# GLA's decay differences as TensorE products with 0/1 masks, instead of scans and subtractions

## The chip, the cores and the metric

The kernel runs on one core of a Trainium2 chip. The metric is the device time of one execution in microseconds (us). Five engines work side by side: PE (TensorE, matmuls), DVE (VectorE), ACT (ScalarE), POOL (GpSimd) and SP, which only issues DMAs. Each takes its instructions in the order in which they stand in its own queue and waits at the head of that queue until its operands are there. TensorE's clock has two levels, 1.2 and 2.4 GHz; the profile gives the share of full speed that was granted.

## The reference, cut to what matters

Two layers of a hybrid backbone run over 384 tokens (128 context tokens, 256 latent ones). Each layer is a feed-forward part, a token mixer with three branches (Mamba-2 SSD, GLA, RWKV-7), and a second feed-forward part. The change is in the GLA branch. It has 4 heads with 64 key and 128 value channels, runs forward and backward, and works in chunks of 64 tokens:

```
lg = log_sigmoid(lr @ gla_gk_w[d] + gla_gk_b[d]) / 16        # a log decay per token and key channel
bc = cumsum(lg, within the chunk)
A[t, s] = sum_k q[t, k] * k[s, k] * exp(bc[t, k] - bc[s, k])  for s <= t
q_dec = q * exp(bc);  k_dec = k * exp(bc[last] - bc)
S_next = exp(bc[last]) * S + k_dec^T v                        # state from chunk to chunk
o = A v + q_dec S
```

The backward scan does the same on reversed tokens, and the two outputs are added.

## The kernel before, in words

Activations are feature-major: a tile holds 128 features by 384 tokens, so two GLA heads lie in one tile and the four heads make two head pairs (`hp`). The weights of the large products are split into a high and a low part (`wh`, `wl`: ACT casts, DVE subtracts) and every product of a 128x128 block is three matmuls of 128x384. In the mixer these read `psd<-mhh,wh` while the input is projected, and `psd<-ob,wh` while a branch's output goes through its output weights; each of the three branches (`w_rw_o`, `w_gla_o`, `w_ssd_o`) has 96 of them, and what PSUM then holds is gated into `merged` by DVE.

`mixer_` (L754) first projects and runs RWKV-7. Then `gla_decays` (L1733) makes the log decays, between the last projections. `scans` (L811) then runs GLA and SSD side by side in lanes that `pace` (L897) interleaves: `states(0)`, `states(1)` and `levels` of `gla` (L1701), and the lanes of SSD. The 96 products of `w_rw_o` are put between their steps; a further lane adds those of `w_gla_o` once GLA is done, and those of `w_ssd_o` come after all of it. `pace` orders the steps by a running model of each engine's time, and a scheduler then sets the final order, so that any new cost moves many instructions.

In GLA, `gla_decays` makes for each head pair and direction a product with the gate weights (`gk`, into PSUM), Abs, Exp and Ln on ACT, two steps on DVE (`gdm`), and a scan on DVE (`b`, one of four tiles) that sums the log decays within each chunk. `gla_states` (L1777) takes two exponentials of it (`qe`, `ke`), multiplies them by q and k (`glqk`), and carries the states `gS` from chunk to chunk.

`gla_levels` (L1832) makes the matrix A without large exponents. It halves the chunk six times. A level takes, for each block of 2H tokens, the pairs (t, s) on different sides of the block's middle, and measures both decays from that middle. Per head pair and level that is four differences into `gD` (two of 128x192 on DVE, two on POOL), one exponential of 128x768 on ACT, one product with q on DVE, one with k on POOL, twelve 64x64 matmuls, and a masked copy of 128x384 on DVE (`gA<-kt,psm`) which writes this level's pairs into A. The diagonal needs no decay.

`gla_output` (L1880) adds A times v and the state terms, and normalises. The matmuls of all these take PSUM from one pool of five banks (`psm`), the large products from another of two (`psd`). All mixer instructions bear line L275, that of the recorder through which they are issued, so they are told apart by their tiles. The lines that build a level's operands are these:

```
nc.vector.tensor_tensor(out=DQ[:, :, 1], in0=f4[:, :, 1], in1=mf, op=ALU.subtract)
nc.gpsimd.tensor_tensor(out=DK[:, :, 0], in0=mf, in1=f4[:, :, 0], op=ALU.subtract)
nc.scalar.activation(out=DD, in_=DD, func=AF.Exp, scale=1.0 / 16)
nc.vector.tensor_mul(out=DD[:, 0], in0=DD[:, 0], in1=q)
nc.gpsimd.tensor_mul(out=DD[:, 1], in0=DD[:, 1], in1=k)
```

## Time and profile before

| what | value |
|---|---|
| median of three runs | 2456.63 us (2456.47 to 2457.42) |
| the profiled execution, device time | 2458.13 us |
| its span in the trace | 2456.4 us, so 1.73 us lie outside it |
| mean granted TensorE clock | 0.97 of full speed |
| PE busy | 2311.0 us of the span (94%) |
| DVE busy | 1760.4 us (72%) |
| ACT busy | 1107.7 us (45%) |
| POOL busy | 509.6 us (21%) |

The profiled execution is 1.50 us above the median. "Busy" counts instructions alone, not DMA issues or semaphores; matmul ends are modelled, and a record can last longer than the distance to the next. The stretch in which GLA and SSD run side by side, from the first SSD and GLA products after the projections to the first products of `w_ssd_o` that run without a break, is 761.8 to 909.6 us in the first layer and 1956.5 to 2109 us in the second. For the first layer it is cut into four parts here: part 1, with the `w_rw_o` products (761.8 to 812.5), part 2, the rest of the second head pair's levels (812.5 to 836.8), part 3, the second head pair's states and outputs (836.8 to 857), and part 4, the rest of SSD, with the `w_gla_o` products (857 to 909.6).

### The profile page before, as it was taken

The page shows a single profiled execution, that of the slowest core. Times are in us where ns is not written, and L with a number is a line of the kernel's source. Part 1 is how long each engine was busy: PE and PEld are TensorE (multiplying, and loading weights), DVE is VectorE, ACT ScalarE, POOL GpSimd, SP SyncE. Part 2 cuts the span into 40 slices and gives each one's busy share as a digit, 9 for nine tenths or more (in the row PEclk, how much of TensorE's full clock was granted, in tenths as well). Part 3 has the DMA queues.
Part 4 walks back from the last instruction along what each step waited for, and adds up shares of the span by engine and source line. Part 5 has one row for each costly group of instructions (what it writes and reads, how often), then busy time and mean ns, then how long its engine had stood idle before and what let it go on. Part 6 is the DMA issues. An engine that isn't in the chain of part 4 may idle for free. (4 is left out here: it accounts for less than half of the span.)

```text
span 2456.4 us, 48779 instructions
## 1 busy us (share of the span) xinstructions
PE 2311.0 (94%) x19825; PEld 2132.9 (87%) x19825; DVE 1760.4 (72%) x3152; ACT 1107.7 (45%) x2015; POOL 509.6 (21%) x582
## 2 busy tenths in 40 slices
PE   6999899899998879999999999989999988999998
PEld 4999897888887669999999999978888766899998
DVE  3967769786658787868486877896767597885433
ACT  3533346354436445543345334744544544463322
POOL 3100024112215541100120001441212265220000
PEclk8999999999999989999999999989999988999999
DMA  9767554334425226667455766433433430554432
GB/s 304 239 201 210 171 156 111 95 96 124 115 83 143 62 73 202 179 189 219 130 183 165 229 211 163 137 83 104 115 106 107 121 113 16 175 180 131 129 117 80
DMA packets 501663, 354.14 MB, mean 144 GB/s; under 512 B 40035, under 2 KB 479985, under 8 KB 500927
## 3 DMA queue, kind: packets, MB, share of 16 engines
q1 hardware_dynamic: 496288, 337.44, 46.8%
q0 software_dynamic: 3680, 6.18, 1.2%
q10 hardware_dynamic: 1471, 7.41, 0.8%
q8 instruction: 155, 2.54, 0.4%
q14 instruction: 69, 0.57, 0.1%
HBM read 326.59 MB, written 24.38 MB: 143 GB/s over the span
## 5 line engine op out<-in xcount | busy, mean ns | idle before, releaser
L649 ACT CAST wh<-wraw 128x1024 fp32r<-128x1024 f32 (+2 forms) x296 | 280.1, 956 | 587.5 <-issue 332.4
L650 DVE TENSOR_TENSOR wl<-wraw,wh 128x1024 fp32r<-128x1024 f32 (+2 forms) x296 | 330.4, 1124 | 220.5 <-ACT wh L649 220.2
L662 PE MATMUL psm<-xh,wl 128*128 128x384 f32 (+1 forms) x896 | 305.2, 341 | 6.0 <-DVE wl L650 6.0
L660 PE MATMUL psm<-xh,wh 128*128 128x384 f32 (+1 forms) x896 | 306.4, 342 | 0.7 <-DVE xh L608 0.7
L661 PE MATMUL psm<-xl,wh 128*128 128x384 f32 (+1 forms) x896 | 304.2, 339 | 0.0
L275 DVE TENSOR_TENSOR wl<-wraw,wh 128x512 fp32r<-128x512 f32 x324 | 241.7, 758 | 84.2 <-ACT wh L275 77.4
L275 PE MATMUL psd<-mhh,wh 128*128 128x384 f32 x848 | 293.3, 347 | 6.1 <-DVE sb L275 3.4
L275 PE MATMUL psd<-mhl,wh 128*128 128x384 f32 x848 | 296.5, 350 | 2.6 <-DVE mhl L275 2.6
L275 PE MATMUL psd<-mhh,wl 128*128 128x384 f32 x848 | 295.3, 348 | 1.3 <-issue 1.3
L275 ACT CAST wh<-wraw 128x512 fp32r<-128x512 f32 x324 | 190.2, 614 | 166.9 <-PE psd L275 112.5
L536 DVE SCALAR_TENSOR_TENSOR aacc<-wada,cs,aacc 128x1024 f32<-128x1024 f32 x210 | 260.7, 1277 | 6.1 <-DMA wada<-in_w_ada_dram 5.7
L662 PE MATMUL psd<-gh,wl 128*128 128x384 f32 x704 | 237.0, 337 | 7.8 <-DVE wl L650 7.8
L660 PE MATMUL psd<-gh,wh 128*128 128x384 f32 x704 | 236.9, 336 | 0.0
L661 PE MATMUL psd<-gl,wh 128*128 128x384 f32 x704 | 236.5, 336 | 0.0
L621 POOL TENSOR_TENSOR acc<-acc,sq 128x384 f32<-128x384 f32 x24 | 28.9, 1205 | 719.6 <-ACT sq L619 710.3
L662 PEld LDWEIGHTS psm<-xh,wl 128*128 128x128 f32 x896 | 169.5, 189 | 8.4 <-DVE wl L650 8.4
L660 PEld LDWEIGHTS psm<-xh,wh 128*128 128x128 f32 x896 | 169.7, 189 | 6.2 <-issue 4.8
L275 PEld LDWEIGHTS psd<-mhl,wh 128*128 128x128 f32 x848 | 161.1, 190 | 15.3 <-issue 6.8
L275 PEld LDWEIGHTS psd<-mhh,wh 128*128 128x128 f32 x848 | 161.2, 190 | 15.0 <-issue 7.2
L660 PE MATMUL psm<-gh,wh 128*128 128x384 f32 x512 | 171.8, 336 | 0.0
L662 PE MATMUL psm<-gh,wl 128*128 128x384 f32 x512 | 171.1, 334 | 0.0
L661 PE MATMUL psm<-gl,wh 128*128 128x384 f32 x512 | 171.0, 334 | 0.0
(454 smaller groups left out, 4902.8 us busy)
## 6 DMA issues: line engine op xcount, KB each, us to landing
wada<-in_w_ada_dram SPq DMA_DIRECT2D x144, 512.0 KB, 4.6
wraw<-in_w_in_dram SPq DMA_DIRECT2D x112, 512.0 KB, 3.8
wraw<-in_ffn_gate_dram SPq DMA_DIRECT2D x88, 512.0 KB, 4.4
wraw<-in_ffn_up_dram SPq DMA_DIRECT2D x88, 512.0 KB, 4.5
wraw<-in_ffn_down_dram SPq DMA_DIRECT2D x64, 512.0 KB, 3.7
wraw<-in_ffn_down_dram SPq DMA_DIRECT2D x32, 384.0 KB, 4.8
gate<-sa SPq DMA_DIRECT2D x48, 192.0 KB, 2.3
gate<-gate SPq DMA_DIRECT2D x48, 192.0 KB, 2.5
```

The lines of the kernel that those rows point to most:

```text
L275: r = f(*a, **k)
L536: nc.vector.scalar_tensor_tensor(out=acc[:, c], in0=w, scalar=x, in1=acc[:, c], op0=ALU.mult, op1=ALU.add)
L621: (nc.vector if k == KD - 1 else nc.gpsimd).tensor_tensor(out=self.acc, in0=self.acc, in1=sq, op=ALU.add)
L649: nc.scalar.copy(out=h[:, x], in_=r[:, x])
L650: nc.vector.tensor_sub(out=lo[:, x], in0=r[:, x], in1=h[:, x])
L660: nc.tensor.matmul(ps, wh, xh, start=first, stop=False)
L661: nc.tensor.matmul(ps, wh, xl, start=False, stop=False)
L662: nc.tensor.matmul(ps, wl, xh, start=False, stop=last)
```

## The change

Log decays are now token-major: a tile holds 128 rows, 64 tokens of a chunk in both directions, by six chunks and 256 channels, split into a high and a low part (`lgh`, `lgl`). Every sum of log decays that GLA needs, from a block's middle to a token or from a token to the chunk's end, is a product of them with a matrix of zeros and ones (`gsum`, 128x1024, a new input that is built beside the constants). `gla_sum` makes one PSUM bank of such sums with four matmuls of 128x256: two chunks, the high and the low part each, and per chunk four groups of 64 columns. ACT takes the exponential out of PSUM.

- `gla_decays` makes twelve products of 64 tokens by 256 channels, four to a bank, instead of four of 128 channels by 384 tokens, adds the bias by DVE from a tile broadcast by DMA (`gkb`), and splits the result. The scans go. POOL issues three DMAs more: `gsum` (512 KB), ahead of the gate weights, and two for `gkb`.
- `gla_inter`, new, makes the decays to the chunk's ends for a head pair: three `gla_sum`, the totals `gtot` by two small copies, and the products with k on DVE and q on POOL, all in one tile `gE`. `gla_states` and `gla_output` read that tile.
- `gla_levels` goes in nine stages per head pair: three pairs of levels, three pairs of chunks. A stage has one `gla_sum`, one exponential of 128x512, a product with q on DVE and one with k on POOL (128x256 each), eight 64x64 matmuls, and two masked copies of 128x128. Three stages are prepared ahead (four buffers of `gD`). The subtractions on DVE and POOL go.

On DVE, while the `w_rw_o` products run, before: `b` are the summed decays, `gA` the matrix A, `merged` the gated output.

```order
L275 COPY_PREDICATED gA<-kt,psm 128x384
L275 TENSOR_TENSOR ke<-ke,glqk 128x384
L275 TENSOR_TENSOR gD<-b_8324 128x24x8
L275 TENSOR_TENSOR gD<-b_8328 128x24x8
L275 COPY_PREDICATED gA<-kt,psm 128x384
L275 TENSOR_TENSOR gD<-b_8324 128x48x4
L275 TENSOR_TENSOR gD<-b_8328 128x48x4
L275 TENSOR_TENSOR gD<-gD,glqk 128x384
L275 SCALAR_TENSOR_TENSOR merged<-gate,psd 128x384
```

On DVE at the same place after: `gE` is the tile of `gla_inter`, `sR` and `sD` belong to SSD.

```order
L294 TENSOR_TENSOR gE<-gE,glqk 128x6x64 x2
L294 COPY_PREDICATED gA<-kt,psm 128x128
L294 TENSOR_TENSOR gD<-gD,glqk 128x4x64
L294 COPY_PREDICATED gA<-kt,psm 128x128
L294 SCALAR_TENSOR_TENSOR merged<-gate,psd 128x384
L294 TENSOR_TENSOR sR<-adh,kt 128x512 x2
L294 COPY_PREDICATED gA<-kt,psm 128x128
L294 SCALAR_TENSOR_TENSOR sD<-kt,dt,sD 128x128
```

The subtractions `gD<-b` are gone, each 128x384 masked copy has become pieces of 128x128, and the multiply is 128x4x64.

On PE, where SSD's first products `ssi` and `ad` stand, before: `gD` are a level's 64x64 matmuls, `psd<-ob` the `w_rw_o` products.

```order
L275 MATMUL psm<-gD 64x64 x12
L275 MATMUL psm<-kt,ke 64x64 x12
L275 MATMUL psd<-ob,wh 128x384
L275 MATMUL psm<-kt,ke 64x64 x12
L275 MATMUL psm<-kt,ssi 64x128 x8
L275 MATMUL psm<-ad,kt 128x8 x8
L275 MATMUL psm<-gD 64x64 x12
L275 MATMUL psd<-ob,wl 128x384
```

On PE around the same two products after; all 96 `w_rw_o` products now stand ahead of this place.

```order
L294 MATMUL psm<-gD 64x64 x8
L294 MATMUL psm<-gsum,lgh 128x256
L294 MATMUL psm<-gsum,lgl 128x256
L294 MATMUL psm<-kt,ssi 64x128 x8
L294 MATMUL psm<-ad,kt 128x8 x8
L294 MATMUL psm<-gsum,lgh 128x256
L294 MATMUL psm<-gsum,lgl 128x256
L294 MATMUL psm<-gD 64x64 x8
```

SSD's first products have moved from the first levels of head pair 0, 29 of the 96 `w_rw_o` products into the stage, to the last level stages of head pair 1. The new products stand between the old ones, four to a stage.

On ACT at the end of the decays, before: `sa` are gates that are then stored by DMA, `gde` the decays' exponentials, `wh` casts of weights.

```order
L275 CAST wh<-wraw 128x512
L275 ACTIVATE gde<-gde 128x384
L275 ACTIVATE sa<-psd 128x384
L275 ACT_TABLE_LOAD
L275 ACTIVATE gde<-gde,eps 128x384
L275 CAST wh<-wraw 128x512 x3
L275 ACT_TABLE_LOAD
L275 ACTIVATE sa<-psd 128x384
L275 CAST wh<-wraw 128x512 x2
L275 ACTIVATE sD<-kt,dt 128x128 x4
```

On ACT there after: `lgh` are the casts to the high part, `ob` the input of the `w_rw_o` products.

```order
L294 ACTIVATE sa<-psd 128x384
L294 CAST lgh<-gdm 128x512
L294 ACT_TABLE_LOAD
L294 ACTIVATE gde<-gde,eps 128x512
L294 ACT_TABLE_LOAD
L294 ACTIVATE sa<-psd 128x384
L294 CAST lgh<-gdm 128x512
L294 CAST ob<-ro 128x384
L294 CAST wh<-wraw 128x512 x3
L294 ACTIVATE gE<-psm 128x512
```

Before, three casts of weights and nothing of GLA stood between the last decay and the last `sa`; now the last cast of `lgh`, one of `ob` and the casts of weights stand behind that `sa`.

The diff, cut where the functions of before are printed above:

```diff
+def gla_sums():
+
+
+    r, t = np.arange(64)[:, None], np.arange(64)[None]
+    m = np.zeros((2, 64, 1024), np.float32)
+    for lev in range(6):
+        h = 32 >> lev
+        mid = t // (2 * h) * (2 * h) + h
+        late = t >= mid
+        x = 128 * lev
+        m[0, :, x:x + 64] = late & (r >= mid) & (r <= t)
+        m[1, :, x:x + 64] = ~late & (r >= t) & (r < mid)
+        m[0, :, x + 64:x + 128] = ~late & (r > t) & (r < mid)
+        m[1, :, x + 64:x + 128] = late & (r >= mid) & (r < t)
+    m[0, :, 768:832], m[0, :, 832:896] = r <= t, r > t
+    m[1, :, 896:960], m[1, :, 960:1024] = r >= t, r < t
+    return m.reshape(128, 1024)
 
...
@@ -1713,18 +1736,20 @@
         def states(d):
             for hp in range(2):
                 p = P[hp]
+                yield from wait(lambda: hp == 0 or P[0].done)
                 if d == 0:
+                    yield from self.gla_inter(gp, hp, q[:, hp, :], k[:, hp, :], b, p)
                     p.vt = yield from self.gla_values(gp, v[:, 2 * hp:2 * hp + 2, :])
-                yield from wait(lambda: p.vt is not None and (hp == 0 or P[0].done))
-                yield from self.gla_states(l, gp, hp, d, q[:, hp, :], k[:, hp, :], b[hp, d], p)
+                yield from wait(lambda: p.vt is not None)
+                yield from self.gla_states(l, gp, hp, d, p)
                 if d == 0:
                     yield from wait(lambda: p.A is not None and 1 in p.states)
                     yield from self.gla_output(gp, p, o[:, 2 * hp:2 * hp + 2, :], gn)
 
         def levels():
             for hp in range(2):
-                P[hp].A = yield from self.gla_levels(gp, q[:, hp, :], k[:, hp, :], b[hp, 0], b[hp, 1])
-                P[hp].gs = gp.tile([128, 2, T], F32, tag="gD", bufs=3, name="ggs")
+                P[hp].A = yield from self.gla_levels(gp, hp, q[:, hp, :], k[:, hp, :], b)
+                P[hp].gs = gp.tile([128, 2, T], F32, tag="ggs", bufs=1, name="ggs")
...
 
     def gla_decays(self, l, gp, tp, b):
         nc = self.nc
+        b.parts = [gp.tile([128, 6, 256], F32R, name=n) for n in ("lgh", "lgl")]
+        b.sums = gp.tile([128, 1024], F32R, name="gsum")
+        nc.gpsimd.dma_start(out=b.sums, in_=self.I['sums'].bitcast(F32R))
         gk = tp.tile([128, 2, 256], F32, name="gk")
-        nc.gpsimd.memset(gk[64:96], 0.0)
+        nc.gpsimd.memset(gk[64:128], 0.0)
+        bias = tp.tile([128, 256], F32, name="gkb")
         for d in range(2):
             nc.gpsimd.dma_start(out=gk[64 + 16 * d:80 + 16 * d, d, :], in_=self.I['gla_gk_w'][l, d])
-
...
+
+        em = []
+        for j in range(3):
+            ps = self.psm()
+            for c in range(2):
+                x = 64 * (2 * j + c)
+                for d in range(2):
+                    nc.tensor.matmul(ps[HS[d], 256 * c:256 * c + 256], self.misc[64:128, x:x + 64], gk[64:128, d, :], start=True, stop=True)
+            e, m = (tp.tile([128, 2, 256], F32, tag=n, bufs=3, name=n) for n in ("gde", "gdm"))
+            nc.vector.tensor_tensor(out=m, in0=ps.rearrange("p (c k) -> p c k", c=2), in1=bias.unsqueeze(1).to_broadcast([128, 2, 256]), op=ALU.add)
+            nc.scalar.activation(out=e, in_=m, func=AF.Abs)
+            nc.scalar.activation(out=e, in_=e, func=AF.Exp, scale=-1.0)
+            em.append((e, m))
+            yield self.soon()
+        for j, (e, m) in enumerate(em):
+            nc.scalar.activation(out=e, in_=e, func=AF.Ln, bias=self.eps[:, 2:3])
+            nc.vector.scalar_tensor_tensor(out=m, in0=m, scalar=0.0, in1=e, op0=ALU.min, op1=ALU.subtract)
+            h, r = (x[:, 2 * j:2 * j + 2, :] for x in b.parts)
+            nc.scalar.copy(out=h, in_=m)
+            nc.vector.tensor_sub(out=r, in0=m, in1=h)
+
+    def gla_sum(self, b, hp, j, x, out):
+
+        nc = self.nc
+        ps = self.psm()
+        for c in range(2):
+            for n, g in enumerate(b.parts):
+                nc.tensor.matmul(ps[:, 256 * c:256 * c + 256], g[:, 2 * j + c, 128 * hp:128 * hp + 128], b.sums[:, x:x + 256], start=(n == 0), stop=(n == 1))
+        nc.scalar.activation(out=out, in_=ps.rearrange("p (c s t) -> p c s t", c=2, s=4), func=AF.Exp, scale=1.0 / 16)
+
+    def gla_inter(self, gp, hp, q, k, b, p):
+
+        nc = self.nc
+        E = gp.tile([128, 6, 4, 64], F32, tag="gE", bufs=1, name="gE")
+        for j in range(3):
+            self.gla_sum(b, hp, j, 768, E[:, 2 * j:2 * j + 2])
+            yield self.soon()
+        p.tot = gp.tile([128, 6, 2], F32, tag="gtot", bufs=2, name="gtot")
+        for d in range(2):
+            nc.scalar.copy(out=p.tot[:, :, d], in_=E[:, :, 2 * d, 63 if d == 0 else 0])
+        p.E = E.rearrange("p c (d x) t -> p c d x t", d=2)
+        q, k = (x.rearrange("p (c t) -> p c t", t=64) for x in (q, k))
+        for d in range(2):
+            nc.vector.tensor_mul(out=p.E[:, :, d, 1], in0=p.E[:, :, d, 1], in1=k)
+        p.ready = self.ck.done
+        for d in range(2):
+            nc.gpsimd.tensor_mul(out=p.E[:, :, d, 0], in0=p.E[:, :, d, 0], in1=q)
 
     def gla_values(self, gp, v):
...
-    def gla_states(self, l, gp, hp, d, q, k, b16, p):
+    def gla_states(self, l, gp, hp, d, p):
...
+        yield p.ready
         kt = gp.tile([128, NC, 64], F32, tag="gkt", bufs=2, name="gkt")
         ps = self.psm()
         for c in range(NC):
             for hs in HS:
-                nc.tensor.matmul(ps[hs, 64 * c:64 * c + 64], f[hs, 64 * c:64 * c + 64], self.k(K_ID64, 64)[hs], start=True, stop=True)
+                nc.tensor.matmul(ps[hs, 64 * c:64 * c + 64], p.E[hs, c, d, 1], self.k(K_ID64, 64)[hs], start=True, stop=True)
...
-                    nc.vector.scalar_tensor_tensor(out=nxt, in0=cur, scalar=e[:, 64 * c + x:64 * c + x + 1], in1=ps[:, 0:128], op0=ALU.mult, op1=ALU.add)
+                    nc.vector.scalar_tensor_tensor(out=nxt, in0=cur, scalar=p.tot[:, c, d:d + 1], in1=ps[:, 0:128], op0=ALU.mult, op1=ALU.add)
...
-    def gla_levels(self, gp, q, k, bf, bb):
+    def gla_levels(self, gp, hp, q, k, b):
 
         nc = self.nc
         NC = T // 64
         A = gp.tile([128, NC, 64], F32, tag="gA", bufs=2, name="gA")
-
-        def operands(lev):
+        qk = [x.rearrange("p (c t) -> p c t", t=64) for x in (q, k)]
+
+        def operands(lev, j):
             self.ck.done = self.ck.pe
...
-            nc.vector.tensor_tensor(out=DQ[:, :, 1], in0=f4[:, :, 1], in1=mf, op=ALU.subtract)
-            nc.vector.tensor_tensor(out=DQ[:, :, 0], in0=b4[:, :, 0], in1=mb, op=ALU.subtract)
-            nc.gpsimd.tensor_tensor(out=DK[:, :, 0], in0=mf, in1=f4[:, :, 0], op=ALU.subtract)
-            nc.gpsimd.tensor_tensor(out=DK[:, :, 1], in0=mb, in1=b4[:, :, 1], op=ALU.subtract)
-            nc.scalar.activation(out=DD, in_=DD, func=AF.Exp, scale=1.0 / 16)
-            nc.vector.tensor_mul(out=DD[:, 0], in0=DD[:, 0], in1=q)
-            nc.gpsimd.tensor_mul(out=DD[:, 1], in0=DD[:, 1], in1=k)
-            return DD[:, 0], DD[:, 1], self.ck.done
-
-
-        levels = (6, 0, 1, 2, 3, 4, 5)
-        nxt = q, k, 0
-        for n, lev in enumerate(levels):
-            Q, K, t = nxt
-            if n < 6:
-                nxt = operands(levels[n + 1])
+            E = gp.tile([128, 2, 4, 64], F32, tag="gD", bufs=4, name="gD")
+            self.gla_sum(b, hp, j, 128 * lev, E)
+            E = E.rearrange("p c (l x) t -> p x c l t", l=2)
+            for i, eng in enumerate((nc.vector, nc.gpsimd)):
+                eng.tensor_mul(out=E[:, i], in0=E[:, i], in1=qk[i][:, 2 * j:2 * j + 2].unsqueeze(2).to_broadcast([128, 2, 2, 64]))
+            return E, self.ck.done
+        stages = [(lev, j) for lev in (0, 2, 4) for j in range(3)]
+        nxt = deque([operands(*stages[0])])
+
...
+        for n, (lev, j) in enumerate(stages):
+            while len(nxt) < 3 and n + len(nxt) < len(stages):
+                nxt.append(operands(*stages[n + len(nxt)]))
+                yield 0
+            E, t = nxt.popleft()
             yield t
-            ps = self.psm()
-            for c in range(NC):
-                x = 64 * c
-                for hs in HS:
-                    nc.tensor.matmul(ps[hs, x:x + 64], K[hs, x:x + 64], Q[hs, x:x + 64], start=True, stop=True)
-            m = self.k(K_GM + 64 * lev, 64).unsqueeze(1).to_broadcast([128, NC, 64])
-            p3 = ps[:, 0:T].rearrange("p (c t) -> p c t", c=NC)
-            if lev == 6:
-                nc.vector.tensor_tensor(out=A, in0=p3, in1=m, op=ALU.mult)
-            else:
-                nc.vector.copy_predicated(out=A, mask=m.bitcast(mybir.dt.int32), data=p3)
+            ps = self.psm()[:, 0:256].rearrange("p (l c t) -> p l c t", l=2, c=2)
+            for i in range(2):
+                for c in range(2):
+                    for hs in HS:
+                        nc.tensor.matmul(ps[hs, i, c], E[hs, 1, c, i], E[hs, 0, c, i], start=True, stop=True)
+            for i in range(2):
+                nc.vector.copy_predicated(out=A[:, 2 * j:2 * j + 2], mask=mask(lev + i, 2).bitcast(mybir.dt.int32), data=ps[:, i])
         return A
 
...
-                            terms.append((sts[d][c][hs, vs], qd[d][hs, cc]))
+                            terms.append((sts[d][c][hs, vs], p.E[hs, c, d, 0]))
```

## Rows read from the trace of the kernel before

**Rows 1.** The page's first part: each engine's busy time, share and instructions.

```profile
PE 2311.0 (94%) x19825; PEld 2132.9 (87%) x19825; DVE 1760.4 (72%) x3152; ACT 1107.7 (45%) x2015; POOL 509.6 (21%) x582
```

**Rows 2.** Windows: from:to, us, busy per engine, PE clock, DMA share, GB/s.

```profile
740.00:761.80 21.80, 21.80 (x100) 16.66 (x99) 18.44 (x32) 19.55 (x31) 9.66 (x14) 1.00 0.56 131
761.80:812.50 50.70, 42.36 (x581) 37.06 (x580) 47.32 (x90) 23.32 (x43) 30.93 (x37) 0.93 0.46 132
812.50:836.80 24.30, 17.70 (x211) 13.21 (x212) 20.82 (x30) 15.08 (x29) 15.59 (x15) 0.86 0.23 72
836.80:857.00 20.20, 17.46 (x278) 13.91 (x276) 13.43 (x29) 7.30 (x20) 11.34 (x12) 1.00 0.10 27
857.00:909.60 52.60, 38.42 (x204) 30.64 (x204) 45.94 (x73) 24.94 (x48) 25.83 (x20) 0.87 0.22 62
1956.50:2109.00 152.50, 121.03 (x1268) 98.42 (x1263) 128.73 (x222) 71.69 (x140) 84.43 (x84) 0.87 0.29 83
```

**Rows 3.** Timeline, ACT and PE: start, us, instruction, [idle before it, releaser].

```profile
767.37 1.28 ACT L275 ACT_TABLE_LOAD   x1 [4.03 <-DMA gate<-sa]
...
878.33 0.69 PE L275 MATMUL psd<-ob,wh 128*128 128x384 f32 x1 [3.86 <-DVE ob L275]
```

**Rows 4.** DVE groups by form, 740 to 912 us: busy, mean ns, idle before.

```profile
L275 DVE TENSOR_TENSOR gD<-b 128x192 f32<-128x192 f32 x24 | 14.5, 642 | 0.0
L275 DVE TENSOR_TENSOR sR<-adh,kt 128x512 fp32r<-128x512 f32 x12 | 14.2, 1194 | 1.7 <-PE psm L275 1.7
L275 DVE SCALAR_TENSOR_TENSOR sD<-kt,dt,sD 128x128 f32<-128x128 f32 x24 | 10.5, 476 | 0.5 <-ACT sD L275 0.5
L275 DVE TENSOR_TENSOR gD<-gD,glqk 128x384 f32<-128x384 f32 x12 | 9.6, 801 | 2.3 <-ACT gD L275 2.3
L275 DVE COPY_PREDICATED gA<-kt,psm 128x384 f32<-128x384 int32 x12 | 7.0, 582 | 0.3 <-PE psm L275 0.3
...
L275 DVE TENSOR_TENSOR sE<-sE,scb 128x512 f32<-128x512 f32 x6 | 6.7, 1111 | 3.9 <-ACT sE L275 3.9
L275 DVE TENSOR_TENSOR sE<-sE,sD 128x512 f32<-128x512 f32 x6 | 5.1, 857 | 0.0
L275 DVE TENSOR_TENSOR_SCAN b<-kt,gdm 128x384 f32<-128x384 f32 x4 | 4.5, 1132 | 0.0
L275 DVE TENSOR_TENSOR ke<-b 128x384 f32<-128x384 f32 x4 | 4.1, 1024 | 0.0
L275 DVE TENSOR_TENSOR ke<-ke,glqk 128x384 f32<-128x384 f32 x4 | 3.8, 939 | 0.0
L275 DVE TENSOR_TENSOR gdm<-gdm,gde 128x384 f32<-128x384 f32 x4 | 2.5, 634 | 0.2 <-ACT gde L275 0.2
L275 DVE TENSOR_TENSOR sx<-sx,sz 128x256 f32<-128x256 f32 x6 | 2.5, 416 | 0.0
L275 DVE COPY gS<-psm 128x128 f32<-128x128 f32 x4 | 1.0, 278 | 0.0
```

**Rows 5.** DVE, one tile in both layers: ns min/median/max, first to last.

```profile
L275 DVE TENSOR_TENSOR gD<-b x48: 334/501/2954, 771.8 to 2015.3; 128x192 f32<-128x192 f32 x48
L275 DVE TENSOR_TENSOR gD<-gD,glqk x24: 543/659/1356, 774.1 to 2017.7; 128x384 f32<-128x384 f32 x24
```

**Rows 6.** POOL groups by form, 755 to 905 us.

```profile
L275 POOL TENSOR_TENSOR gD<-gD,glqk 128x384 f32<-128x384 f32 x12 | 15.5, 1302 | 10.2 <-ACT gD L275 10.1
```

**Rows 7.** ACT groups by form, 755 to 912 us.

```profile
L275 ACT ACTIVATE gD<-gD 128x768 f32<-128x768 f32 x12 | 10.0, 845 | 16.4 <-DVE gD L275 12.3 <-PE psd L275 2.9 <-POOL gD L275 1.2
...
L275 ACT ACTIVATE sct<-psm 128x512 f32<-128x512 f32 x8 | 4.5, 594 | 3.7 <-PE psm L275 3.7
```

**Rows 8.** Timeline of PE, in two places.

```profile
749.24 1.55 PE L275 MATMUL psm<-misc,gk 32*128 32x384 f32 x4
...
760.96 0.34 PE L275 MATMUL psd<-mhh,wl 128*128 128x384 f32 x1
761.14 0.34 PE L275 MATMUL psd<-mhh,wh 128*128 128x384 f32 x1
```

More of the change, by code (lines that the diff above doesn't have):

```diff
@@ L1882, in gla_output @@
         nc = self.nc
-        vt, A, sts, qd = p.vt, p.A, p.states, p.qd
+        vt, A, sts = p.vt, p.A, p.states
         sq = []
@@ L2209 @@
     arrays, I = {}, {}
-    for name in _INS + ['consts']:
-        a = constants() if name == 'consts' else np.ascontiguousarray(inputs[name])
+    made = dict(consts=constants, sums=gla_sums)
+    for name in _INS + list(made):
+        a = made[name]() if name in made else np.ascontiguousarray(inputs[name])
         arrays[f"in_{name}_dram"] = a
```

61 lines of the change are left out of this document (15 added, 46 removed).

## The prediction

> **What bounds the kernel now.** I read the page's first part first: PE is busy 94% of the span, so outside a few stretches a microsecond saved on DVE is worth nothing, and one added to PE costs itself [rows 1]. Then I looked for the stretch that the change touches. The windows show it [rows 2]. Just ahead of it, from 740 to 761.8 us, PE is busy all 21.80 us and DVE 18.44: PE sets that stretch, and in it the decays are made. From 761.8 to 909.6 us, where GLA and SSD run, DVE is busy 47.32 of 50.70, 20.82 of 24.30, 13.43 of 20.20 and 45.94 of 52.60 us, in all 127.5 of 147.8; PE is busy 115.9, so it stands idle 31.9 us. The second layer's stretch is alike: PE 121.03 and DVE 128.73 of 152.50, so PE is idle there for 31.5. These 63 us are all that less DVE work can win. The third view, the waits, shows where PE's idle time comes from [rows 3]: in part 4 PE waits 3.86 us for DVE's `ob`, and at the start of part 1 ACT waits 4.03 us for the store of an earlier gate, which holds the weight casts behind it. So in this stretch DVE is late in parts 1, 2 and 4, and in part 3 neither is (DVE 66%, PE 86%).
>
> **The change: DVE.** Per layer these go [rows 4]: 24 differences (14.5 us), 12 multiplies of 128x384 (9.6), 12 masked copies (7.0), 4 scans (4.5), 4 differences and 4 multiplies for `ke` (4.1 and 3.8). Of the new ones, the trace does not show a 128x256 multiply beside a POOL one. Alone it is near the `sx` row, 416 ns for the same size; the old `gD` multiply has a mean of 801 ns against a least time of 543 [rows 4, 5], since POOL multiplies from the same exponential at that moment, so I scale: 416 x 801/543 = 614, say 0.61 us. The bounds are 0.41 (no contention) and 1.28: POOL's own 128x384 multiply takes 1302 ns [rows 6], two thirds of it is 0.87, and 0.41 + 0.87 is a DVE that starts after POOL has ended. A masked copy of 128x128 lies between the `gS` copy out of PSUM, 278 ns, and two thirds of 582, that is 388; I take 0.32. Eighteen multiplies are 11.0, 36 copies 11.5, and 4 `gE` multiplies at the `ke` price 3.8 us.
>
> By where they stand in the order, with part 1 ending at the `merged` step that ended it before: part 1 loses 20 differences (12.8), 9 multiplies (7.2), 8 masked copies (4.7), a scan (1.1), one `gdm` difference (0.6), two `ke` differences and two `ke` multiplies (2.0 and 1.9) and small SSD work of about 1.9 at the `sx` price, 32.2 us; it gains 18 copies (5.8), 12 multiplies (7.3) and 2 of `gE` (1.9), 15.0. Its DVE work falls by 17.2 us by means. Means count the overlap of neighbouring records twice: all of part 1's DVE instructions sum to 56.3 us by them and it took 50.70 [rows 2], a factor of 0.90. So part 1 is 15.5 shorter by DVE's own work, 35.2 us. Two things then hold DVE back. The order puts the last `lgh` cast, an `ob` cast and weight casts behind the `sa` that waited 4.03 us for the store [rows 3]; before, GLA's work did not hang on that wait, now the first `gsum` does: +4.0. And the stretch starts late, see PE: +2. That is 41 us.
>
> **PE.** Each bank of sums has 4 products of 128x256, and there are 24 banks a layer (18 stages, 6 for `gE`): 96 products. Two 128x384 matmuls of the projection, at full clock, start 0.174 us apart [rows 8] (761.14 less 760.96); by columns that is 0.116 for 256, and 0.174 is the other bound. With 0.145 it is 13.9 us a layer (11.1 to 16.7), which neither removal nor DVE can pay for unless it falls into PE's idle time. In part 1 there are 60 of them, 8.7 us, against 8.34 us of PE's idle time there. PE busy was 42.36, so if nothing left part 1 it would need 51; but its records last longer than their distance (0.34 against 0.174), and SSD's first products and the second pair's `ke` products have gone elsewhere. So PE's floor lies between 39 and 51, and I take 42, just above DVE's 41. Part 1: 50.7 to 42, -8.7 us.
>
> In the stretch before, which PE fills, 12 `gk` products replace 4. Four records, two products, took 1.55 us [rows 8]. By columns 12 of 256 take 12 x 0.78 x 2/3 = 6.2 against 3.1, +3.1 at most; 0 at least, if part of that was pauses; I take 1.5. Their weights now stand behind the 512 KB of `gsum` on POOL's queue, whose landing I have no row for: between nothing and the 4.03 of the other wait on a DMA, 0.5, near the lower, since PE had products of the projection to run in the meantime. Start: +2 a layer, from 0 to 7. The decays' DVE work there stays about what it was: nine steps of 128x512 at twice the `sx` price, 7.5 us, for four scans (4.5) and eight `gdm` steps of which each takes near 0.63 (5.0).
>
> **Parts 2 to 4.** Part 2 loses 4 differences, 3 multiplies, 4 copies and a `ke` difference, 8.3 us, and hands on a part of SSD's first decay stage: two `sR` (2.4), two `sE` steps (2.0), four `sD` (1.9), 6.3 in all; it gains 18 copies, 6 multiplies and 2 of `gE`, 11.3, and about 1 us of small SSD work. Net -2.3, by its own factor (22.1 by means, 24.30 measured) -2.5. Part 3 keeps its products; PE has more to do in it, but a part of that has run in part 2: 0, up to +5.9, which is PE at 0.145 for the 40 or so sums that part 2 may leave over. Part 4 takes over what part 2 hands on. In the order, two of SSD's output stages stood before the end of part 3, and now none stands before the last GLA output. That is 6.3 us, with two `sx` multiplies (0.8), two sums on PSUM as long (0.8) and one weight split that slips in (0.9) 8.8 by means, and 9.3 by the factor of part 4 (49.7 by means, 52.60 measured). DVE was idle 6.7 us in it and may take up 4 of them, so +5.3 to +9.3; I take +7.3.
>
> **ACT and POOL.** ACT gives up 12 exponentials of 128x768 (10.0) and eight shorter ones for `ke` and `qe`, for 24 of 128x512 out of PSUM, 594 ns by the `sct` row, 14.3 [rows 7]. It is about even, and ACT is busy less than half of parts 1 and 4. POOL gives up its 24 differences, which no engine waits for at the end; that is worth nothing by itself.
>
> **Sum.** Per layer -8.7 - 2.5 + 0 + 7.3 = -3.9; the start's +2 is in part 1, whose 41 and 42 both count from 761.8 us. Two layers: -7.8. The profiled execution, 2458.1 (span 2456.4 and 1.7 around it), becomes 2450.3. It was 1.5 above the median of the runs, so a median of 2449 us. What of it is sure is the DVE work that leaves; what is not is whether SSD's late start takes it back.
>
> A page bears on the multiply. The trace shows the least 128x384 multiply at 543, the median at 659 and the longest at 1356 ns [rows 5]. The Trainium skill, "SBUF — State Buffer", section "SBUF: two separate sides", says that VectorE and GpSimd share a port pair which whoever starts first holds for its whole instruction, and that a VectorE operation with two SBUF inputs falls under it when GpSimd reads SBUF. By that rule the new pair, both released by the same exponential, would run one after the other. The median of 659 agrees with it in part only: most are not held for a whole POOL multiply. It is rival D.
>
> **Rivals.** B, DVE sets everything: the stall and the late start are hidden by three prepared stages and PE has room. Part 1 gives its 15.5, part 2 2.5, part 4 takes 5.3: -12.7 a layer, 2431 us. For it: DVE is busy 93% of part 1. Against it: PE's 8.7 us of new products there.
>
> C, slower, SSD a stage late: SSD is the longest chain once GLA is quicker, and its `ssi` and `ad` products stand behind all of `w_rw_o`. Parts 1 and 2 give back only 7.5, part 3 costs its 5.9 and part 4 its 9.3: +7.7 a layer, 2472 us. It decides once parts 1 and 2 together give less than the 15.2 that 3 and 4 would take. For it: part 4 already runs on DVE at 87%, and nothing of GLA is left there to save. Against it: in parts 2 and 3 together PE was idle 9.3 of 44.5 us and DVE 10.3 [rows 2], so there is room to catch up.
>
> D, the lock: each new multiply waits for POOL's, 1.28 us each instead of 0.61. Part 1 has 12 x 0.67 x 0.90 = 7.2 more DVE work, 48 against PE's 42, and part 2 6 x 0.67 x 1.1 = 4.4 more: -2.5 + 1.9 + 7.3 = +6.7 a layer, 2470 us.
>
> E, no change: PE's floor in part 1 is 46, the middle of what I could bound. Part 1 gives 4.7, part 2 2.5, part 4 takes 7.3: 2457 us. For it: the sums add 8.7 to an engine that had 8.3 free.
>
> **How the numbers follow.** The forecast has a chance of 0.50, B 0.12, C 0.18, D 0.06, E 0.14. The forecast's own range is 2441 to 2458. 0.2% is 4.9 us, about what a measurement of this kernel can tell from no change, so below 2451.7 is faster, above 2461.5 slower. Faster: 0.72 of the forecast, all of B, a little of E, 0.50. Slower: C, D, and a little of the rest, 0.26. The range of 2434 to 2470 leaves out most of B and half of C.
>
> **What would show it.** In the profile after: part 1, to the last `w_rw_o` product, near 42 us and not 50 or 35; `gsum` products 0.12 to 0.17 us apart; the `gD` multiply near 0.61 and the `gA` copy near 0.32; the wait of the last `sa` followed by a wait of DVE for `lgh`; the first `w_ssd_o` product some 4 us earlier in the stretch than before, with SSD's `sE` and `sx` steps in the last 60 us; and PE's idle time in the stretch down by about 18 us a layer, as it has 14 more to do in 4 less. I am wrong if the stretch ends later than before, or if part 1 is shorter by more than 12 us.

## The result, and the profile after

The changed kernel takes 2472.57 us (median of 4 runs, 2468.96 to 2475.34) against 2457.03 us for the kernel before (4 runs, 2456.47 to 2458.24). The ratio is 1.006 with a 95% interval of 1.0047 to 1.0072: slower by 15.5 us, where 8 us less were forecast, and outside the forecast range. The profiled execution of the changed kernel was the fastest of its four; its span is 10.7 us longer than that of before. Other chips gave the kernel before 2456.7 to 2459.2 us, so below each kernel is told by its ratio to runs of before on its own chip.

Windows of the changed kernel: the stretch ahead, parts 1 to 4 (to the end of the last idle time before `w_ssd_o`), and ten microseconds ahead of the second layer's stretch. The columns are those of [rows 2].

```profile
738.00:759.80 21.80, 21.48 (x111) 16.66 (x111) 15.53 (x28) 17.95 (x27) 6.04 (x8) 1.00 0.53 152
759.80:810.50 50.70, 43.66 (x527) 38.34 (x527) 34.30 (x75) 21.92 (x44) 19.53 (x24) 0.93 0.54 140
810.50:830.60 20.10, 20.09 (x310) 16.87 (x311) 17.22 (x38) 13.80 (x27) 9.82 (x10) 1.00 0.19 57
830.60:847.50 16.90, 16.90 (x260) 12.87 (x259) 13.10 (x23) 9.57 (x22) 10.06 (x11) 1.00 0.05 14
847.50:914.50 67.00, 46.05 (x274) 38.67 (x274) 58.46 (x89) 29.11 (x59) 36.95 (x28) 0.86 0.20 55
1940.00:1950.00 10.00, 8.27 (x28) 4.06 (x28) 4.08 (x7) 4.17 (x6) 0.00 (x0) 0.83 0.85 270
```

Against [rows 2], part 1 is as long as before (50.7 us) though DVE is busy 34.30 us in it instead of 47.32. Part 2 is 4.2 us shorter and part 3 3.3 us, both with PE busy throughout. Part 4 is 14.4 us longer (52.6 before). GLA's last output product comes 9 us earlier than before (847.0 against 856.5 us), in a stretch that starts 2 us earlier, and SSD after it takes longer. The stretch ends at 914.5 us instead of 909.6, which is one of the two signs of being wrong that the forecast named. PE's idle time in it falls from 31.9 to 28.0 us, not by 18.

ACT of the changed kernel around the start of part 1 (columns as in [rows 3]):

```profile
760.25 1.28 ACT L294 ACT_TABLE_LOAD   x1
761.54 0.49 ACT L294 ACTIVATE sa<-psd 128x384 f32<-128x384 f32 x1
...
762.85 1.66 ACT L294 CAST wh<-wraw 128x512 fp32r<-128x512 f32 x3
771.56 0.60 ACT L294 ACTIVATE gE<-psm 128x512 f32<-128x512 f32 x1 [7.05 <-DMA gate<-sa]
```

The wait of 4.03 us in front of the last `sa` is gone: nothing stands in brackets there. In its place the first `gE` waits 7.05 us for the store of an `sa` (7.97 us in the second layer), and the weight casts behind it wait too.

PE of the changed kernel: the first sums, then the end of that wait, then the gate products of the second layer.

```profile
759.69 0.28 PE L294 MATMUL psm<-gsum,lgh 128*128 128x256 f32 x1
759.81 0.28 PE L294 MATMUL psm<-gsum,lgl 128*128 128x256 f32 x1
...
772.21 0.58 PE L294 MATMUL psm<-gsum,lgh 128*128 128x256 f32 x1 [6.32 <-ACT gE L294]
...
1941.82 0.61 PE L294 MATMUL psm<-gk,misc 64*64 64x256 f32 x2 [1.53 <-DMA gk<-in_gla_gk_w_dram]
```

A sum product takes 0.12 us (759.81 less 759.69), not 0.145; [rows 8] gave the bounds. PE stands idle 6.32 us at the wait. In the second layer the gate weights come late, and the clock granted in the ten microseconds from 1940 on is 0.83 of full speed, where it was 1.00 before.

DVE groups of the changed kernel, 740 to 915 us (columns as in [rows 4]):

```profile
L294 DVE TENSOR_TENSOR sR<-adh,kt 128x512 fp32r<-128x512 f32 x12 | 16.8, 1418 | 1.5 <-PE psm L294 1.5
L294 DVE TENSOR_TENSOR gD<-gD,glqk 128x256 f32<-128x256 f32 x18 | 12.3, 688 | 9.6 <-ACT gD L294 9.5
L294 DVE COPY_PREDICATED gA<-kt,psm 128x128 f32<-128x128 int32 x36 | 10.5, 296 | 3.1 <-PE psm L294 2.7
...
L294 DVE TENSOR_TENSOR gE<-gE,glqk 128x384 f32<-128x384 f32 x4 | 3.6, 909 | 0.0
```

The prices of the new instructions were about right: 688 ns for 0.61 us, 296 for 0.32, 909 for 0.94. SSD's `sR` has grown from 1194 to 1418 ns.

### The profile page after: what moved, and what is told of

Same layout as the page of the kernel before. It is cut to its first block, busy times and chain, and to the rows that moved or that the text cites. A ratio compares the mean times of both kernels' runs of the same rounds, so it can differ in the third digit from the quotient of the medians.

```text
span 2467.1 us, 49234 instructions
## 1 busy us (share of the span) xinstructions
PE 2323.5 (94%) x20049; PEld 2149.3 (87%) x20049; DVE 1744.4 (71%) x3150; ACT 1112.8 (45%) x2031; POOL 490.3 (20%) x552
```

## The experiments

Theories in turn: S (SSD starts late, and that is the loss), P (PE's sums), W (the wait for the store).

**ssd_first.**
```diff
-        self.pace(lanes + more + [after_gla()], 10000)
+        self.pace(more + lanes + [after_gla()], 10000)
```


> The changed kernel with one line changed: the SSD lanes stand ahead of the GLA lanes in the list that is paced, so SSD's first products come among the first w_rw_o products again instead of behind all 96. Nothing is left out. Theory S (SSD starts late and its stages, not GLA, end the stretch): the last SSD sum pss<-ssq, 147 us into the stretch in the changed kernel (909.1 us), comes 8 to 15 us earlier and the time falls from 2472 to 2445 to 2458 us. Rival P (the 96 sums a layer on PE lengthen the stretch): PE has the same work, so 2470 us or more. Rival W (the 7 us wait of the first gE exponential for a gate's store, in each layer, is what is lost): that wait stays, so 2468 us or more, unless SSD's work fills it.

Measured 1.0097 (1.0082 to 1.0112): slower still. SSD's last sum came at 862.0 instead of 909.1 us, but GLA's last output product at 895.5 instead of 847.0, and the last product of the branches' outputs 4 us later. To put SSD first does not win the loss back.

**place.**
```diff
         gn = gp.tile([128, 2], F32, name="gn")
+        self.vts = [gp.tile([128, T // 64, 128], F32, tag="gvt", bufs=2, name="gvt")]
```
(and `gla_values` takes its first tile from there). 

> The changed kernel with the tile gvt allocated ahead of gE, so that gE and gD no longer lie on the memory of the staging tile sa and need not wait for its store. Nothing is left out. Rival W: the waits of 7.05 us (first layer) and about 7.3 us (second) go from ACT, PE's 6.32 and 7.26 us of idle time go with them, and the time falls by 10 to 14 us to 2459 to 2463. Theory S: the stretch begins earlier, but SSD still starts behind the w_rw_o products; these come earlier by what the wait took, so most of it shows too, 6 to 12 us, 2461 to 2467. Rival P: PE's work is the same and PE was idle in part 1 for other reasons too; 2 to 6 us at most.

Measured 1.0009 (0.9996 to 1.0022), the forecast of W: some 12 us back. In the built programs `gE` had lain at byte 87296 of each partition and was 6144 bytes long, so it covered the staging tiles `sa` at 88800 and 90336; in place `gvt`, written later, lies at 87296, and `gE` at 93440, behind them. ACT of place:

```profile
764.95 1.66 ACT L294 CAST wh<-wraw 128x512 fp32r<-128x512 f32 x3
766.51 0.59 ACT L294 ACTIVATE gE<-psm 128x512 f32<-128x512 f32 x1
```

No wait is left. Its four parts:

```profile
761.40:806.90 45.50, 42.84 (x544) 37.75 (x542) 36.11 (x77) 22.64 (x46) 21.01 (x24) 1.00 0.60 156
806.90:826.40 19.50, 19.49 (x295) 16.34 (x294) 16.63 (x38) 13.20 (x26) 9.77 (x10) 1.00 0.19 59
826.40:843.30 16.90, 16.90 (x260) 12.87 (x259) 13.10 (x23) 9.62 (x22) 10.06 (x11) 1.00 0.04 14
843.30:909.70 66.40, 44.40 (x276) 37.10 (x275) 58.47 (x90) 29.12 (x59) 37.00 (x28) 0.88 0.21 59
```

Parts 1 to 3 take 81.9 us instead of 95.2. Part 4 takes 13.8 us more, all of the 13.3 gained.

The second layer's balance is another. From its first products to the wait before `w_ssd_o` the stretch takes 152.0 us before, 153.3 in the changed kernel and 145.8 in place (in the first layer 147.9, 154.8 and 148.0). The 6 us that place gains there are lost ahead of it, mostly in code that both kernels share: its second stretch starts 9.5 us later than that of before, and from 1900 to 1950 us the granted clock is 0.93 instead of 1.00. These are single executions, and they scatter: before_late below, whose time is that of before, has 146.6 us in that stretch.

**before_late.**
```diff
+        def held(lane):
+            while not pairs[0].done:
+                yield None
+            yield from lane
-        self.pace(lanes + more + [after_gla()], 10000)
+        self.pace(lanes + [held(x) for x in more] + [after_gla()], 10000)
```


> The kernel before, with the SSD lanes held back until the first GLA head pair is done, so that SSD's first products stand behind all 96 w_rw_o products, as they do in the changed kernel. No product with masks, nothing left out. Theory S: slower by 10 to 25 us, 2467 to 2482, with the first pss<-ssq at 850 us or later (841.4 before). Rivals P and W: SSD's start is no cost by itself; within 4 us of 2457.

Measured 1.0003 (0.9991 to 1.0014). SSD's first products now stand at 819.9 us instead of 782.9, behind the last `w_rw_o` step, and its first sum comes at 843.7 instead of 841.4. In the kernel before SSD's late start costs nothing; S is refuted.

**no_low** (in `gla_sum`, `b.parts` becomes `b.parts[:1]`). 

> The changed kernel with the products of the low part lgl left out of every sum (48 of 96 sum products a layer), so decays have the high part's precision alone. Rival P: 48 x 0.12 to 0.145 us a layer, 11 to 14 us less, 2459 to 2461. Theory S: SSD starts behind these products too, but part of them runs while ACT or DVE are waited for; 3 to 8 us less, 2464 to 2469. Rival W: the waits at the start stay; 0 to 4 us less.

Measured 1.0175 (1.0159 to 1.0192): less work, 27 us slower than the changed kernel. The planner, which no longer counts the products, had moved SSD's steps (its first products from 821.4 to 797.0 us), so this alone decides nothing.

**place_gk** (the `gsum` DMA moved behind the loop that loads `gk` and `gkb`). 

> The kernel of place, with POOL's DMA of the masks gsum issued behind those of the gate weights gk and the bias gkb instead of ahead of them. Nothing is left out. What the first batch left: place took back 13 of the 15.5 us, so the wait for the gate's store was most of the loss, and SSD's start alone (before_late) cost nothing. Theory G: PE's wait for gk in the second layer (1.53 us, with a lower clock behind it, some 4 us in all) goes, 2 to 5 us less than place, 2453 to 2458 by place's own 2459. Rival: gk lands as late, since the gate products of a layer are asked for behind other DMAs anyway, and gsum then comes late for the first sums; 0 to 3 us more than place.

Measured 0.999 (0.9976 to 1.0003), 1.9 per mille or 4.7 us below place, with intervals that overlap. In its trace no gate product waits for `gk`, and the loads of `gk` land 2.3 us after their issue at the median instead of 5.1 in place. The 4.7 us are within theory G's range, but they are not shown to be that wait: place's own trace has only 0.60 us of PE's waiting for `gk`, in the first layer.

**place_nosd.**
```diff
-                nc.vector.scalar_tensor_tensor(out=D[:, j, :], in0=self.k(K_GE), ...)
+                self.ck.count('vector', 'scalar_tensor_tensor', D[:, j, :], (), ...)
```


> The kernel of place with the four DVE steps sD of each SSD stage left out (24 a layer, 11.4 us of DVE by the trace of place), so the backward decay of SSD is missing from its products; the planner still counts them, so the order on PE stays. Theory D (part 4 follows DVE, which is busy 61.0 of its 71.6 us): 18 of the 24 stand in part 4, 7 to 8 us a layer there, so 14 to 18 us less, 2442 to 2446. Rival K (part 4 follows a chain of waits through PE, ACT, POOL and DVE of one SSD stage after the other): the steps are in that chain once each, so 4 x 0.45 us a stage, but ACT's sD and POOL can take their place; 4 to 10 us less, 2450 to 2456. Rival P (PE at its lower clock, 0.86, sets part 4): 0 to 3 us less.

Measured 0.9997 (0.9988 to 1.0006), 3 us below place. Part 4 of place_nosd:

```profile
845.40:909.10 63.70, 43.22 (x276) 36.26 (x275) 50.60 (x70) 29.02 (x59) 36.86 (x28) 0.91 0.23 66
```

DVE has 7.9 us less in it than in place, the part is 2.7 us shorter. An engine that is busy 88% of a part need not set it. The time lies just below theory K's range and in that of theory P, and the intervals overlap; pg_dve below speaks against P for this part.

**place_nolow** (as no_low on place, with the planner still counting the products). 

> The kernel of place with the low part's products left out of each sum (48 a layer), while the planner still counts them, so that the rest of the order stays as it is; no_low, which also changed the order, took 27 us more than the changed kernel. Parts 2 and 3 of place have PE busy 36.4 of 36.4 us. Theory P2 (PE's sums set parts 2 and 3): about 24 products fewer there by 0.12 us, 3 us a layer, and 2 in part 1: 8 to 10 us less than place, 2449 to 2452. Rival C (the clock: with less work PE's granted clock falls, 0.79 in part 4 of no_low against 0.85): 0 to 15 us more than place, with a lower clock in the windows.

Measured 1.0045 (1.0032 to 1.0058): 9 us slower than place with 96 products fewer. Part 2 of the second layer, place_nolow:

```profile
2013.60:2034.20 20.60, 18.73 (x265) 15.40 (x262) 17.67 (x38) 12.10 (x24) 9.18 (x10) 0.83 0.18 56
```

and place:

```profile
2009.70:2029.30 19.60, 19.55 (x298) 16.40 (x295) 16.82 (x38) 13.30 (x26) 9.59 (x10) 1.00 0.20 58
```

PE, with idle time in it, is granted 0.83 of full speed, a mean over stretches at 2.4 and 1.2 GHz, instead of 1.00, and the part is no shorter. P does not hold as it was put: to leave half of the sums out saves nothing here. It does not price the sums at an unchanged clock (see what stays open).

**pg_mid** (`more[1:3]` ahead of `lanes` on place_gk). 

> The kernel of place_gk with two of SSD's four lanes, its start and its states, ahead of the GLA lanes in the paced list, and its fronts and outputs behind them as before. Nothing is left out. Theory R (the DVE time that GLA gives back lies idle in parts 1 to 3 because SSD's work is not there to take it; part 4 then has all of it): SSD's preparation moves into part 1, where DVE is idle 9 us, part 4 shrinks by 4 to 8 us a layer, 2445 to 2453. Rival: as ssd_first, what SSD takes in part 1 delays GLA by as much and the w_gla_o products with it; 2458 to 2468.

Measured 1.0033 (1.0022 to 1.0044), 10 us slower than place_gk, as the rival said.

**after_again** (no edit). 

> The changed kernel itself once more, on the same chip as the three below, so that what place took back is measured on one more chip. All theories: 1.004 to 1.007 of the kernel before, 10 to 18 us slower, with the wait of about 7 us in front of the first gE exponential in both layers.

Measured 1.0055 (1.0037 to 1.0072): the loss is there again on another chip, and so are the waits of the first `gE` for the store, 15.4 us in the two layers.

**before_nosub** (`...` stands for the planner's count of the two differences, which stays).
```diff
-            nc.vector.tensor_tensor(out=DQ[:, :, 1], in0=f4[:, :, 1], in1=mf, op=ALU.subtract)
-            nc.vector.tensor_tensor(out=DQ[:, :, 0], in0=b4[:, :, 0], in1=mb, op=ALU.subtract)
...
-            nc.scalar.activation(out=DD, in_=DD, func=AF.Exp, scale=1.0 / 16)
-            nc.vector.tensor_mul(out=DD[:, 0], in0=DD[:, 0], in1=q)
+            nc.scalar.activation(out=DD[:, 1], in_=DD[:, 1], func=AF.Exp, scale=1.0 / 16)
+            nc.vector.tensor_mul(out=DD[:, 0], in0=q, in1=q)
```


> The kernel before with VectorE's two differences of each level left out (24 a layer, 14.5 us) and the exponential taken over the k half alone; q is multiplied by itself in place of the decay. So A is wrong on its query side; the planner counts the differences still. Theory F (the forecast's premise: in parts 1 and 2 the stretch follows DVE): 14.5 x 0.9 less a layer, 20 to 26 us in all, 2432 to 2438. Rival K (what GLA gains in parts 1 and 2 is given back in part 4, where SSD's stages follow one another): the levels end 8 to 12 us earlier a layer, the stretch ends 0 to 4 us earlier, 2450 to 2458.

Measured 0.9988 (0.9978 to 0.9998): 2.9 us. Its parts 1, 2 and 3:

```profile
761.80:808.20 46.40, 40.95 (x550) 35.45 (x546) 41.87 (x71) 19.03 (x41) 30.02 (x36) 0.96 0.53 156
808.20:820.40 12.20, 9.51 (x155) 8.30 (x154) 6.23 (x11) 7.45 (x15) 6.68 (x9) 0.86 0.32 99
820.40:854.90 34.50, 27.60 (x336) 20.81 (x334) 24.05 (x42) 14.47 (x33) 20.09 (x18) 0.80 0.05 15
```

Parts 1 and 2 give 16.4 us, and part 3 takes 14.3 of them back at once (20.2 before). Theory F, the premise of the forecast, is refuted in the kernel before itself: K was right on the sum and wrong on the part, which is part 3 and not part 4. DVE is busy 24.05 us in part 3 instead of 13.43, since more of SSD's steps and of GLA's output stand there now, and PE is granted 0.80 of full speed instead of 1.00; which of the two sets its length is not shown.

**place_noadl** and **before_noadl** (the same edit on place and on the kernel before; the products with `r[2 * d + 1]` go as well).
```diff
-                for a, eng in ((self.adh, nc.vector), (self.adl, nc.gpsimd)):
+                for a, eng in ((self.adh, nc.vector),):
```


> The kernel of place with the low part of SSD's decays left out: POOL's 12 sR products a layer (16 us of POOL, 12 of them in part 4), half of the 40 sR matmuls, and with them the wait for sR buffers, since a stage then takes two of the four. Theory K (part 4 follows the chain of one SSD stage after the other: sR buffers free, sR, matmuls, exponential, two sE steps): 2 to 3 us a stage, 10 to 18 us less than place, 2442 to 2450. Rival D (it follows the amount of DVE work): place_nosd took 11 us of it out of part 4 and gained 3, so here, where only DVE's sR grow shorter, 4 us or less. Rival P (PE): 20 sums of 128x512 less a layer, 4 us a layer at most.

> The kernel before with the same left out as in place_noadl. Theory K: SSD's chain sets part 4 here too, but two of its six stages already stand ahead of it; 6 to 12 us less than before, 2445 to 2451. Rival: in the kernel before, GLA's DVE work holds parts 1 and 2 and SSD's stages there are free; 0 to 5 us less.

Measured 0.9928 (0.9911 to 0.9945), 20 us below place, and 0.9888 (0.9868 to 0.9907), 27 us below before. Part 4 of place_noadl:

```profile
846.80:897.90 51.10, 36.91 (x233) 29.11 (x232) 46.74 (x80) 28.49 (x59) 25.83 (x19) 0.94 0.26 72
```

It is 15.3 us shorter than in place, with 11.7 us less of DVE, 11.2 less of POOL and 7.5 less of PE, where 7.9 us of DVE alone had given 2.7. SSD's last five sums in place, the first and the last:

```profile
864.74 0.61 PE L294 MATMUL pss<-ssq,kt 128*128 128x128 f32 x4
...
904.16 0.71 PE L294 MATMUL pss<-ssq,kt 128*128 128x128 f32 x4 [1.50 <-ACT ssq L294]
```

and in place_noadl:

```profile
864.74 0.71 PE L294 MATMUL pss<-ssq,kt 128*128 128x128 f32 x4 [2.00 <-ACT ssq L294]
...
892.82 0.71 PE L294 MATMUL pss<-ssq,kt 128*128 128x128 f32 x4 [1.37 <-ACT ssq L294]
```

The same four stages take 39.4 and 28.1 us. SSD's stages set the end in both kernels, and in the kernel before by more than was expected. The edit takes work from three engines, so it does not say which of them held the stages; the next runs take that up.

**before_sr6** and **pg_sr6** (`tag="sR", bufs=6`; on place_gk with two buffers of `gD`). 

> The kernel before with six buffers of sR instead of four, nothing else changed and nothing left out. Theory B (the chain of an SSD stage is held by the buffers: sR of the next stage waits until PE has used all four): DVE's and POOL's waits for PE in front of sR (14.6 and 9.8 us over both layers) shrink, 4 to 10 us less than before, 2447 to 2453. Rival L (it is held by the time of POOL's own sR, 1.3 us each, two to a stage, and what DVE's lose beside them): within 3 us of before.

> The kernel of place_gk with six buffers of sR, paid for by two of gD instead of four. Nothing left out. Theory B: 6 to 12 us less than place_gk, 2446 to 2452, since all six SSD stages follow one another here. Rival L: within 3 us of place_gk. A third: with two gD buffers GLA's levels lose their look-ahead and parts 1 and 2 grow by 2 to 6 us a layer.

Measured 0.9992 (0.9982 to 1.0002) and 1.0013 (1.0003 to 1.0023). In the kernel before the buffers hold nothing. pg_sr6 is 2 per mille slower than place_gk, so nothing is gained there either, but it has two buffers of `gD` fewer, and the third theory (the levels' look-ahead) may have hidden a gain.

**pg_dve** and **before_dve** (the same edit on place_gk and on before).
```diff
-                for a, eng in ((self.adh, nc.vector), (self.adl, nc.gpsimd)):
+                for a, eng in ((self.adh, nc.vector), (self.adl, nc.vector)):
```


> The kernel of place_gk with the low part of sR made by VectorE instead of POOL, so VectorE has 12 products of 128x512 more a layer (0.68 us each without a neighbour) and POOL 12 fewer. Nothing left out. Rival L: a stage's four sR take 4 x 0.68 = 2.7 us in a row instead of 2.8 side by side with POOL, and DVE's other work runs beside a quieter POOL: 2 to 8 us less than place_gk, 2450 to 2456. Theory B: as long as four buffers are there, within 3 us. Theory D (amount of DVE work): 8 us a layer more on DVE, 5 to 12 us slower.

> The kernel before with the low part of sR made by VectorE instead of POOL, as in pg_dve, which was 0.9961 of the kernel before. Nothing left out. Theory M (the products with masks pay once SSD's stages no longer hold the end, because VectorE then has room for the low sR): here VectorE is busy already in parts 1 and 2, so 0 to 5 us less than before at most, 2452 to 2459, and pg_dve stays 4 to 10 us ahead of it. Rival N (pg_dve's gain is SSD's alone and has nothing to do with the masks): 7 to 12 us less than before here too.

Measured 0.9961 (0.9947 to 0.9975), 2448.42 us, and 0.9926 (0.991 to 0.9942), 2441.6 us. DVE does 12 products of 128x512 more a layer and both kernels are faster. The tile `sR` on DVE of before_dve, both layers (columns as in [rows 5]):

```profile
L275 DVE TENSOR_TENSOR sR<-adh,kt x24: 676/686/1764, 765.5 to 2061.1; 128x512 fp32r<-128x512 f32 x24
L275 DVE TENSOR_TENSOR sR<-adl,kt x24: 666/684/1757, 766.1 to 2062.2; 128x512 fp32r<-128x512 f32 x24
```

and in the kernel before:

```profile
L275 POOL TENSOR_TENSOR sR<-adl,kt x24: 1034/1316/1489, 758.9 to 2084.8; 128x512 fp32r<-128x512 f32 x24
L275 DVE TENSOR_TENSOR sR<-adh,kt x24: 677/1458/1773, 766.6 to 2083.9; 128x512 fp32r<-128x512 f32 x24
```

The two DVE products take 686 and 684 ns at the median, one after the other; with the low part on POOL, DVE's took 1458 at the median. So DVE is no busier for its 12 products more: in place_gk the two layers' stretches take 147.3 and 146.9 us with DVE busy 121.3 and 122.0, in pg_dve 143.6 and 144.5 us with DVE busy 122.5 and 122.3, and PE is as busy in both. Before_dve beats both kernels and pg_dve with all work done. Rival N was right that the gain needs no masks; the 18 us are more than its 7 to 12. The planner counts the moved products on their new engine, so in both kernels the order of other steps moves too, and the gain is that of the whole edit.

**pg_half** (`nc.vector if d else nc.gpsimd`). 

> The kernel of place_gk with the low part of sR made by VectorE for the backward direction and by POOL for the forward one. Nothing left out. Theory L as it stands after pg_dve: half the pairs still run beside each other, so half the gain, 3 to 7 us less than place_gk, 2451 to 2455. Rival: one POOL product beside three of VectorE is the best split of a stage, 2444 to 2449. A third: any POOL product beside VectorE's costs all of it, 2456 or more.

Measured 0.9978 (0.9966 to 0.9989), between place_gk and pg_dve: near half the gain, as L said, though the interval overlaps that of place_gk.

## Why the prediction was wrong

**The premise.** The step "DVE is late in parts 1, 2 and 4", from which each microsecond of DVE work was turned into one of time, is the one that failed. Busy shares of 93% and 86% [rows 2] were read as a bound. Before_nosub takes 14.5 us of that work a layer (by the means of [rows 4]; the first layer's windows hold 9.4 less) and gains 1.5: the levels end sooner, and part 3 takes the time back. So the time saved on DVE in parts 1 and 2 does not reach the end of the stretch. DVE was busy partly because its `sR` lasted 1458 ns beside POOL instead of 686.

**Part 1, 42 us.** Measured 50.7. The term of +4.0 for the wait of `sa` was mis-sized and put on the wrong wait, and it stood in DVE's 41 alone, while PE's 42 held no wait. The wait of `sa` vanished; the new one, 7.05 us for ACT and 6.32 for PE, comes from where a tile lies, which neither the order nor the diff shows. Over two layers it is most of the measured loss, some 12 of 15.5 us (place). Without it part 1 is 45.5 us with PE busy 42.84, so the work in PE's floor of 42 was about right, and 2.7 us of idle time were missing.

**The start, +2 a layer.** Not shown. PE waits 0.32 us for `gk` in the first layer and 1.53 and 0.20 in the second, but in after_again 0.40 in the second alone. The first layer's stretch starts 2 us earlier than before, and 0.5 us later in after_again, so the term is within the scatter of single executions.

**Parts 2 and 3, -2.5 and 0.** Better: -4.2 and -3.3. PE is busy throughout both. That it sets them is not shown: with half of the sums left out, part 2 of the second layer was no shorter, at a lower clock (place_nolow).

**Part 4, +7.3 within 5.3 to 9.3.** Measured +14.4, with place +13.8. The work that moves there was counted nearly right: two `sR`, two `sE` steps and four `sD` were to come, and three, two and six came, so that DVE is busy 12.5 us more in it. But it was priced as DVE work, and in part 4 such work is not what sets the time: 7.9 us less of it gave 2.7 (place_nosd), and pg_dve is faster with DVE as busy over the stretch. What the move costs is more runs through the chain of an SSD stage, in which DVE, POOL and PE wait for each other: 9.9 us a stage over the last four of place, 7.0 in place_noadl. How the 14.4 us divide among the steps of that chain is not shown.

**The rivals.** C named 2472 us, and the time is 2472.57; that the numbers meet is luck. A half of its mechanism is there: SSD's stages take back in part 4 what the parts ahead give. The other half is not: it wanted part 3 longer, which is shorter, and SSD's late start costs nothing (before_late). The 12 us that place takes back were a wait that C did not have.

D, the lock, wanted 1.28 us for each new multiply, and the mean is 688 ns. Its mark is there all the same. The multiply in both layers (columns as in [rows 5]), and two pairs with POOL's, in one of which POOL starts first, in the other DVE:

```profile
L294 DVE TENSOR_TENSOR gD<-gD,glqk x36: 410/427/1221, 772.7 to 2030.4; 128x256 f32<-128x256 f32 x36
...
790.19 0.75 POOL L294 TENSOR_TENSOR gD<-gD,glqk 128x256 f32<-128x256 f32 x1 [3.40 <-ACT gD L294]
790.29 0.92 DVE L294 TENSOR_TENSOR gD<-gD,glqk 128x256 f32<-128x256 f32 x1
...
804.18 0.42 DVE L294 TENSOR_TENSOR gD<-gD,glqk 128x256 f32<-128x256 f32 x1 [0.70 <-ACT gD L294]
804.23 0.98 POOL L294 TENSOR_TENSOR gD<-gD,glqk 128x256 f32<-128x256 f32 x1 [0.75 <-ACT gD L294]
```

In the first pair DVE starts second, takes 0.92 us and ends 0.27 after POOL; in the second it starts first and takes 0.42, and POOL's multiply takes 0.98 instead of 0.75. The median of 427 says that in more than half of the pairs DVE did not pay, not that nobody did. What D had wrong is who waits. SSD's `sR` in the kernel before shows the same:

```profile
792.01 1.15 POOL L275 TENSOR_TENSOR sR<-adl,kt 128x512 fp32r<-128x512 f32 x1
792.19 1.52 DVE L275 TENSOR_TENSOR sR<-adh,kt 128x512 fp32r<-128x512 f32 x1
```

DVE's product ends 0.55 us after POOL's, and takes 0.68 alone. The pair takes 1.70 us from first to last, where DVE does two in 1.37. The Trainium skill, "SBUF — State Buffer", section "SBUF: two separate sides", has the mechanism: VectorE with two SBUF inputs and GpSimd reading SBUF exclude each other. The trace agrees: whoever starts second does most of its work after the first has ended.

E, no change, is what remains once both waits are taken away: place_gk, 0.999. Its part 1 of 46 is near the 45.5 of place, but PE, which was to set it, is busy 42.84 us of them, and its parts 2 to 4 are not those measured.

**What stays open.** With SSD's `sR` on DVE the masks cost 3.5 per mille (pg_dve against before_dve, intervals apart), some 8 us. PE is busy 129.4 us of that stretch in the first layer with them and 121.1 without. That these 8 us are the sums' is likely, and was not tried; the two kernels ran on two chips, each against the kernel before.

## What to carry to other kernels

A high busy share shows that an engine works, not that its work sets the end: before counting on a saving, leave the work out on the kernel as it is, or look at whether the next chain (here SSD's stages) can start sooner. New tiles have addresses: ask what lay there, and whether the last reader is a DMA. Two engines put side by side on the same kind of operand can be slower than one of them doing both.

## What the runs showed of the hardware

- Removing PE work made the kernel slower (place_nolow, +9 us; part 2 of the second layer at a granted clock of 0.83 instead of 1.00, and 1 us longer). Not all of it need come from that: ahead of the second layer's stretch, from 1900 us on, the granted clock was 0.88 in place_nolow, 0.93 in place (both to 1950) and 1.00 in place_gk (to 1943), so it differs there between executions.
- A DVE product of 128x512 took 686 ns at the median with POOL's product of the same kind taken away, and 1458 with it; of a pair, the one that started second ended 0.55 us after the first. 12 products more for DVE a layer made the kernel 18 us faster (before_dve).
- Loads of 16 KB issued behind one of 512 KB on POOL's queue landed 5.6 us after their issue at the median, and 2.3 us with the order turned round (place_gk). Behind it they kept PE waiting 1.53 us in the second layer and 0.32 us in the first; in place_gk PE did not wait for them.
